# Attention's probabilities times values: plain float32 on halves of the output partitions, and weight buffers at multiples of 256 bytes

## The chip, the cores and the metric

The kernel runs on one core of a Trainium2 chip. The metric is the device time of one execution in microseconds (us). The kernel before takes 1887.37 us, the median of three runs (1886.77 to 1890.65). Besides these there is one profiled execution, from which every row below comes: it took 1884.77 us, and the profile's span of it, from the first to the last instruction, is 1883.0 us.

## The reference

Two layers of a diffusion transformer work on 256 context tokens and 256 latent tokens of width 1024. Each layer has a token mixer (latent attention with 8 heads beside a long convolution called Hyena) and a channel mixer (a dense SwiGLU in layer 0, top 2 of 8 experts in layer 1). All weights and results are float32. The change is inside attention, for each head of 64 values:

```python
def attend(q, k, v):
    s = jnp.einsum('bqhd,bkhd->bhqk', q, k).astype(jnp.float32) * ATTN_SCALE
    p = jax.nn.softmax(s, axis=-1).astype(v.dtype)
    return jnp.einsum('bhqk,bkhd->bqhd', p, v)        # probabilities times values

mix_ctx = ...   # layer 0 only: context queries attend to the 256 context keys
mix_lat = ...   # both layers: latent queries attend to context and latent keys, 512 in all
x = x + g1 * mix_lat
x = x + g2 * channel_mixer(...)   # layer 1: experts' gate, up (1024 x 2816) and down (2816 x 1024), 8 experts
```

So a head of layer 0 has 256 latent queries over 512 keys and 256 context queries over 256 keys; a head of layer 1 has the latent queries alone.

## The kernel before, in words

**Products.** A large matrix product is done as three matmuls on float32r operands, written by `mm3` (L193 to L196). Each operand stands in SBUF as a high part (the value rounded to float32r) and a low part (the rest); the three are high x high (L194), high x low (L195) and low x high (L196). They run on TensorE (PE), whose rows in the trace carry these line numbers. Plain float32 matmuls go through `mm` (L191); the trace shows each of them as two rows. A row of a matmul reads "out<-the operands", then the tile as moving and stationary sizes: 128x512 is a moving operand of 512 columns, and 128\*128 or 128\*2 the stationary one.

**Splitting.** An operand that comes out of a product is split by `split` (L207 on ScalarE, ACT, writes the high part; L209 on VectorE, DVE, the low part). Weights arrive by DMA in `raw` (or `rawx`) and are split by the class `Stream` (L103 on ACT, L105 on DVE) into weight buffers: `hl`, three tiles in the pool `consts`, and later `hlx`, which lie in slots. `fetch` (L87) starts the DMA on SyncE's queue (SP) when a buffer is free.

**Memory.** SBUF holds, one after the other in each partition, the pool `consts` (constants, `raw`, the three `hl`, small things), then 17 slots of 8 KB, then small tiles. Most activations, and in the expert stage the additional weight buffers `hlx`, `rawx`, lie in slots. Worked out from the tile sizes, `hl0` begins at byte 35,776 of a partition and `raw` at byte 19,392 (both 192 past a multiple of 256), and the slots at byte 66,560, a multiple of 256.

**Attention** (`mixer`, L730 on). Layer 0 works on all 512 tokens at once, layer 1 on the 256 latent ones. The loop over heads is written in the order in which PE runs it: for head h the probabilities are transposed (`probs_T`, L951 in the trace) and split into `pt`; then the scores of a later head; a projection of queries and keys for a later pair of heads; a block of Hyena or gate projection (`next_unit`); and the products with the values (`values`). In layer 0 `values(h)` comes after `next_unit`; in layer 1 `values(h - 1)` comes before it. `values` of head h multiplies a block of 128 value columns, which belong to two heads, as the stationary operand with the head's probabilities, 256 queries, as the moving one: 4 key blocks of 128 times 3 matmuls, and in layer 0 the context queries beside them, 2 blocks times 3. Of the 128 output partitions the 64 that belong to the head are kept. The context probabilities stand in `cq` (`ptc`), the values in `vt`, the result in `oT`.

**Elsewhere.** `mod_first`, at the start of layer 0, has float32 matmuls that write output partitions 0 and 1 (operand `mod`) and 64 and 65 (operands `acc` or `mod`) of one PSUM bank; the program's condition vectors `condT` are their stationary operand, two columns wide. `fw` is the network that makes the Hyena filter, also in float32.

Of the kernel before, what the change touches and what calls it, by code (L numbers as in the profile page):

```python
# [8 lines left out]
F32 = mybir.dt.float32  # L9
F32R = mybir.dt.float32r  # L10
# [125 lines left out]
def trunk(ctx, tc, T, out, dump=None, stop=None):  # L136
    nc = tc.nc
    dump = dump or (lambda *a: None)
    consts = ctx.enter_context(tc.tile_pool(name="consts", bufs=1))
# [6 lines left out]
    def nm(s):  # L146
        uid[0] += 1
        return f"{s}_{uid[0]}"
# [3 lines left out]
    def PS(hold=None):  # L152

        k = next(b for b in banks if b not in held)
        banks.remove(k)
        banks.append(k)
        if hold is not None:
            held.add(k)
            hold.append(k)
        return psum.tile([128, 512], F32, name=nm("ps"), tag=f"bank{k}")  # L160
# [14 lines left out]
    def slot(dtype, shape=None, name="s"):  # L175
        k = free.pop(0)
        t = slots.tile([128] + list(shape or [2048]), dtype, name=nm(name), tag=f"slot{k}")
        return Slot(k, t)

    def drop(*ss):  # L180
        for s in ss:
            free.append(s.k)
# [4 lines left out]
    def f(ap):  # L187
        return ap.bitcast(F32)

    def mm(o, l, r, a, b):  # L190
        pe.matmul(o, l, r, start=a, stop=b)  # L191

    def mm3(o, lh, ll, rh, rl, a, b):  # L193
        pe.matmul(o, lh, rh, start=a, stop=False)  # L194
        pe.matmul(o, lh, rl, start=False, stop=False)  # L195
        pe.matmul(o, ll, rh, start=False, stop=b)  # L196

    def copy(i, o, src):
        if i % 2:
            dve.tensor_copy(o, src)  # L200
        else:
            act.activation(o, src, AF.Copy)

    def split(*parts):

        for h, _, src in parts:
            act.activation(h, src, AF.Copy)  # L207
        for h, l, src in parts:
            dve.tensor_tensor(l, src, f(h), OP.subtract)  # L209
# [70 lines left out]
        return vecs[:, l, a:a + n]  # L280


    consts.tile([128, 8], F32, name="fill")
    raw_t = consts.tile([128, 4, 1024], F32, name="raw")
    hl_t = [consts.tile([128, 2, 1024], F32R, name=f"hl{i}") for i in range(3)]
    ri = [0]
# [333 lines left out]
    def split_dft(raw):  # L620
        s = slot(F32R, [2, 2, 512], "dfts")
        split((s.t[:, 0], s.t[:, 1], raw.t))
        drop(raw)
        return s
# [112 lines left out]
    def mixer(l, hTh, hTl, state, hooks, fsteps, in_q=None):  # L737
        N = 512 if l == 0 else 256
        NS = N // 256
        H, L = hT_views(hTh, hTl)  # L740
        qtab = slot(F32, [4, 512], "qtab")
# [35 lines left out]
        def to_T(toks, nb, nk, gain, dst):  # L777
            for kc in range(nk):
                p = PS()
                for tb in range(nb):  # L780
                    pe.transpose(p[:, tb * 128:(tb + 1) * 128], toks[tb][:, kc * 128:(kc + 1) * 128], ident)
                h, lo = dst(kc)
                g = vcol(l, gain + kc)
                act.activation(h, p[:, :nb * 128], AF.Copy, scale=g)
                dve.scalar_tensor_tensor(lo, p[:, :nb * 128], g, f(h), OP.mult, OP.subtract)
# [6 lines left out]
        for tb in range(4):  # L792
            src = kv_ps[tb][:, 256:288]
# [11 lines left out]
        kt = [slot(F32R, [2, 2, 512], "kt") for _ in range(1 + l)]  # L805
# [36 lines left out]
        def unit(c):  # L842
            p = proj_block(("hy", l, c), N)
            if c >= 8:
                short_conv(p, c, x0[0].t[:, c - 8, :N])
                return
            u = tmp("u", [512], bufs=2)
            short_conv(p, c, u[:, :N])
            if c < 4:
                vbuf[c] = u  # L850
            else:
                pool.tensor_tensor(zv[:, c - 4, :N], vbuf.pop(c - 4)[:, :N], u[:, :N], OP.mult)
# [3 lines left out]
        def next_unit():  # L856
            if units:
                unit(units.pop(0))
# [9 lines left out]
        K = state["K"]  # L868
        cq = Pair(N, "cq")
        to_T(cq_tok, N // 128, 3, V_QN, lambda kc: (cq.h[:, kc, :], cq.l[:, kc, :]))  # L870
        vt = [slot(F32R, [4, 512], "vt") for _ in range(2)]
        wh, wl = (t.rearrange("p (k c) -> p k c", k=2) for t in ws.take(("uv", l)))
        for kb in range(4):
            p = PS()
            for kc in range(2):
                mm3(p, ckv.t[:, 0, kc, kb * 128:(kb + 1) * 128], ckv.t[:, 1, kc, kb * 128:(kb + 1) * 128],
                    wh[:, kc], wl[:, kc], kc == 0, kc == 1)
            split((vt[0].t[:, kb, :], vt[1].t[:, kb, :], p))
        qt = slot(F32R, [2, 2, 512], "qt")
        if l == 0:  # L880
            pts = slot(F32R, [2, 4, 256], "pt")
            pt = [(pts.t[:, 0], pts.t[:, 1])]
        else:
            pt = [[x[i].t[:, :, 256:512] for x in (hTh, hTl)] for i in range(2)]
        oT = Pair(N, "oT")

        def qpart(pr):
# [53 lines left out]

        def probs_T(h):
            res = prob.pop(h)
            pth, ptl = pt[h % len(pt)]
            for half in range(2):
                p = PS()
                p3 = p.rearrange("p (k q) -> p k q", k=2)
                for k in range(2):
                    for i in range(2):
                        kb = half * 2 + k  # L950
                        pe.transpose(p3[:, k, i * 128:(i + 1) * 128], res[i][:, kb * 128:(kb + 1) * 128], ident)  # L951
                split((pth[:, half * 2:half * 2 + 2, :], ptl[:, half * 2:half * 2 + 2, :], p3))
            if l == 0:
                p = PS()
                p3 = p.rearrange("p (k q) -> p k q", k=2)
                for k in range(2):
                    for i in range(2):
                        pe.transpose(p3[:, k, i * 128:(i + 1) * 128], res[2][:, i * 256 + k * 128:i * 256 + (k + 1) * 128], ident)
                split((ptc[0], ptc[1], p3))

        def values(h):
            pr, e = divmod(h, 2)
            pth, ptl = pt[h % len(pt)]
            po = PS()
            c = slice(pr * 128, (pr + 1) * 128)
            for kb in range(4):
                mm3(po[:, 0:256], vt[0].t[:, kb, c], vt[1].t[:, kb, c], pth[:, kb, :], ptl[:, kb, :], kb == 0, kb == 3)
            if l == 0:
                for k in range(2):
                    mm3(po[:, 256:512], vt[0].t[:, 2 + k, c], vt[1].t[:, 2 + k, c], ptc[0][:, k], ptc[1][:, k], k == 0, k == 1)  # L970
            r = slice(e * 64, e * 64 + 64)
            split((oT.h[r, pr, :], oT.l[r, pr, :], po[r, :N]))

        if l == 0:
            ptc = [x[:, 3, :].rearrange("p (k q) -> p k q", k=2) for x in (cq.h, cq.l)]
        pairs = {}

        def gate(n, j):
# [27 lines left out]
        for h in range(8):  # L1006
            probs_T(h)
            if h + ahead < 8:
                scores(h + ahead)
            pr = h // 2 + ahead  # L1010
            if h % 2 == 0 and pr < 4:
                proj_pair(pr)
            if h == 4:
                drop(ckv)
                x0.append(slot(F32, [4, 512], "x0"))
            if h == 6:
                drop(qt, *kt)
                if l == 0:
                    drop(qtab)
                else:  # L1020
                    drop(*cq.s)
                Fraw = load_dft("k_fwd", pool, False)
            if h == 7:
                Fd = split_dft(Fraw)
                zts = [slot(F32R, [4, 512], "zt") for _ in range(NS)]
                zt = [zts[0].t, zts[1].t] if l == 0 else [zts[0].t[:, 0:2], zts[0].t[:, 2:4]]
                z_T()
            if l == 0:
                next_unit()
                values(h)  # L1030
            else:
                if h > 0:
                    values(h - 1)
                next_unit()
        if l == 1:
            values(7)
        drop(*vt)
        if l == 0:
            drop(pts, *cq.s)
        dump(f"oT{l}", oT)  # L1040
        dump(f"z{l}", z)

# [5 lines left out]
        for s in range(NS):  # L1048
            yh, yl = slot(F32R, [2, 2, 512], "Yh"), slot(F32R, [2, 2, 512], "Yl")
            Y.append((yh, yl))  # L1050
            for kb in range(2):
                zs = []
                for cs in range(2):
                    p = PS()
# [17 lines left out]
        for j in range(4):  # L1072
            p = PS()
            for s in range(NS):
                i = 0
# [16 lines left out]
        for j in range(8):  # L1092
            ga, gh = [early.pop(n + str(j)) if j < AHEAD[l] else gate(n, j) for n in ("ga", "gh")]
            wh, wl = (t.rearrange("p (b k c) -> p b k c", b=2, k=4) for t in ws.take(("br", l, j)))
            for b, src, g in ((0, oT, ga), (1, oh, gh)):
                p = PS()
# [4 lines left out]
            q, r = divmod(j, 4)  # L1101
# [46 lines left out]

    setup_vectors()
    starts, rows0 = setup_rows()  # L1150
    consts.tile([128, 8], F32, name="end")
    pads.extend(consts.tile([128, 2, 258], F32, name=f"pad{i}") for i in range(2))
    for t in pads:
        dve.memset(t[:, :, 0:258:257], 0.0)
# [53 lines left out]
    hTh, hTl = hT  # L1208
# [33 lines left out]
    hTh, hTl = new  # L1242
# [26 lines left out]
    def mms(p, w, cols):  # L1269
        for kc in range(8):  # L1270
            mm3(p[:, cols], w[0][:, kc], w[1][:, kc], H(kc)[:, cols], L(kc)[:, cols], kc == 0, kc == 7)
# [69 lines left out]
    for hh in range(2):  # L1341
# [15 lines left out]
        else:  # L1357
# [3 lines left out]
            hTh, hTl = alloc_hT()  # L1361
# [146 lines left out]
    for i in range(2):  # L1508
# [3 lines left out]
        for k in range(4):  # L1512
            c = slice(k * 256, (k + 1) * 256)
# [21 lines left out]
    p = PS()  # L1535
# [197 lines left out]
    for b in range(2):  # L1733
        for k in range(2):
            c = slice(k * 512, (k + 1) * 512)
# [25 lines left out]
```

## Time and profile before

| What | Value |
|---|---|
| runs, median (lowest, highest) | 1887.37 us (1886.77, 1890.65) |
| profiled execution | 1884.77 us |
| its span | 1883.0 us |
| granted TensorE clock, mean | 0.993 |
| PE busy | 1827.4 us (97%) |
| VectorE (DVE) busy | 1473.5 us (78%) |
| ScalarE (ACT) busy | 1097.0 us (58%) |
| GpSimd (POOL) busy | 143.2 us (8%) |
| moved by DMA | 436.35 MB, mean 232 GB/s |

An engine's busy time is the part of the span in which an instruction of it was running. The stages follow one another: setup until about 60 us, layer 0's mixer (its attention loop some 120 to 236 us), the dense feed-forward until about 860 us, layer 1's mixer (attention loop some 900 to 955 us), and the experts from about 1075 us to the end.

### The profile page before, as it was taken

To read this page: it belongs to the slowest core of one execution; us is meant where nothing else is said; L and a number is where in the kernel's file an instruction comes from. 1 tells how busy PE (TensorE), PEld (TensorE's weight loads), DVE (VectorE), ACT (ScalarE), POOL (GpSimd) and SP (SyncE) were. 2 spreads that over 40 slices of the span, in tenths; PEclk is the share of its full clock that TensorE was granted. 3 is DMA by queue.
4 is the path that set the end of the run, shared out by engine and by line. 5 is a ranking of instruction groups with operands and counts; after the bars stand their busy time and mean duration, and the time that the engine had idled before them with its cause. 6 is when DMAs were issued, how large, how long until landed. Compare 5 with 4: busy or idle time off the path is not lost. (4 is left out here: it accounts for less than half of the span.)

```text
span 1883.0 us, 25341 instructions
## 1 busy us (share of the span) xinstructions
PE 1827.4 (97%) x9767; PEld 1537.7 (82%) x9767; DVE 1473.5 (78%) x1705; ACT 1097.0 (58%) x1342; POOL 143.2 (8%) x148
## 2 busy tenths in 40 slices
PE   7999999999999999999999899999999999999997
PEld 2888887898888887788999788888878887888785
DVE  5777778787677667768886789888888897888886
ACT  3766633236233235558865577677677676767674
POOL 1122221000000000001221100000000000000000
PEclk9999999999999999999999899999999999999999
DMA  8322226655566676224468499999999999999994
GB/s 296 105 67 67 79 76 199 193 165 144 172 198 191 213 240 204 84 85 117 119 186 262 147 324 339 334 334 342 368 327 344 347 365 324 352 328 360 342 352 180
DMA packets 292316, 436.35 MB, mean 232 GB/s; under 512 B 9848, under 2 KB 162852, under 8 KB 292188
## 3 DMA queue, kind: packets, MB, share of 16 engines
q1 hardware_dynamic: 288652, 422.52, 66.8%
q0 software_dynamic: 3392, 12.00, 2.0%
q8 instruction: 78, 1.28, 0.3%
q14 instruction: 50, 0.41, 0.1%
q10 hardware_dynamic: 144, 0.14, 0.0%
HBM read 433.58 MB, written 1.05 MB: 231 GB/s over the span
## 5 line engine op out<-in xcount | busy, mean ns | idle before, releaser
L103 ACT ACTIVATE hl<-raw 128x1024 fp32r<-128x1024 f32 (+7 forms) x231 | 188.0, 836 | 279.6 <-PE ps L195 167.5
L194 PE MATMUL ps<-hTh,hl 128*128 128x512 f32 (+1 forms) x800 | 283.0, 354 | 0.0
L195 PE MATMUL ps<-hTl,hl 128*128 128x512 f32 (+1 forms) x800 | 283.0, 354 | 0.0
L196 PE MATMUL ps<-hTh,hl 128*128 128x512 f32 (+1 forms) x800 | 282.2, 353 | 0.4 <-DVE hl L105 0.4
L105 DVE TENSOR_TENSOR hl<-raw,hl 128x1024 fp32r<-128x1024 f32 (+7 forms) x231 | 218.7, 965 | 72.0 <-ACT hl L103 71.4
L103 ACT ACTIVATE hlx<-raw 128x2048 fp32r<-128x2048 f32 x124 | 237.9, 1921 | 54.2 <-DMA raw<-in_moe_w_up_dram 16.9
L194 PE MATMUL ps<-hlx,xT 128*128 128x512 f32 (+1 forms) x576 | 215.4, 374 | 0.0
L196 PE MATMUL ps<-hlx,xT 128*128 128x512 f32 (+1 forms) x576 | 214.3, 372 | 0.0
L439 DVE SCALAR_TENSOR_TENSOR acc<-raw,condT,acc 128x1024 f32<-128x1024 f32 x112 | 143.9, 1307 | 36.1 <-DMA raw<-in_w_mod_dram 35.6
L191 PE MATMUL ps<-hlx,aT 128*128 128x512 f32 x704 | 170.2, 393 | 0.0
L196 PEld LDWEIGHTS ps<-hTh,hl 128*128 128x128 f32 x800 | 150.2, 188 | 22.5 <-DVE hl L105 0.6
L194 PEld LDWEIGHTS ps<-hTh,hl 128*128 128x128 f32 x800 | 150.3, 188 | 21.9
L195 PEld LDWEIGHTS ps<-hTl,hl 128*128 128x128 f32 x800 | 150.2, 188 | 20.9
L105 DVE TENSOR_TENSOR hlx<-rawx,hlx 128x2048 fp32r<-128x2048 f32 x65 | 149.3, 2297 | 15.6 <-ACT hlx L103 15.6
L105 DVE TENSOR_TENSOR hlx<-raw,hlx 128x2048 fp32r<-128x2048 f32 x63 | 144.2, 2288 | 16.7 <-ACT hlx L103 16.4
L105 DVE TENSOR_TENSOR hl<-rawx,hl 128x2048 fp32r<-128x2048 f32 (+1 forms) x63 | 141.9, 2254 | 14.3 <-ACT hl L103 13.6
L191 PEld LDWEIGHTS ps<-hlx,aT 128*128 128x128 f32 x704 | 130.1, 188 | 26.3
L105 DVE TENSOR_TENSOR hl<-raw,hlx 128x2048 fp32r<-128x2048 f32 x61 | 139.6, 2288 | 14.4 <-ACT hlx L103 14.4
L195 PE MATMUL ps<-hl,xT 128*128 128x512 f32 (+1 forms) x384 | 146.0, 380 | 3.0 <-DVE hl L105 3.0
L195 PE MATMUL ps<-hlx,xT 128*128 128x512 f32 (+1 forms) x384 | 145.0, 378 | 3.2 <-DVE hlx L105 3.2
L103 ACT ACTIVATE hlx<-rawx 128x2048 fp32r<-128x2048 f32 x67 | 128.4, 1916 | 32.9 <-DMA rawx<-in_moe_w_up_dram 9.1
L103 ACT ACTIVATE hl<-rawx 128x2048 fp32r<-128x2048 f32 (+1 forms) x63 | 118.8, 1888 | 26.7 <-DMA rawx<-in_moe_w_gate_dram 9.9
(395 smaller groups left out, 3749.0 us busy)
## 6 DMA issues: line engine op xcount, KB each, us to landing
rawx<-in_moe_w_gate_dram SPq DMA_DIRECT2D x44, 1024.0 KB
rawx<-in_moe_w_down_dram SPq DMA_DIRECT2D x43, 1024.0 KB
raw<-in_moe_w_down_dram SPq DMA_DIRECT2D x43, 1024.0 KB
raw<-in_moe_w_up_dram SPq DMA_DIRECT2D x42, 1024.0 KB
rawx<-in_moe_w_up_dram SPq DMA_DIRECT2D x41, 1024.0 KB
raw<-in_moe_w_gate_dram SPq DMA_DIRECT2D x41, 1024.0 KB
raw<-in_w_mod_dram SPq DMA_DIRECT2D x80, 512.0 KB
raw<-in_w_in_dram SPq DMA_DIRECT2D x56, 512.0 KB
```

The lines of the kernel that those rows point to most:

```text
L103: self.nc.scalar.activation(a, r, AF.Copy)
L105: self.nc.vector.tensor_tensor(b, r, a.bitcast(F32), OP.subtract)
L191: pe.matmul(o, l, r, start=a, stop=b)
L194: pe.matmul(o, lh, rh, start=a, stop=False)
L195: pe.matmul(o, lh, rl, start=False, stop=False)
L196: pe.matmul(o, ll, rh, start=False, stop=b)
L439: dve.scalar_tensor_tensor(a, raw, condT[:, kc, c:c + 1], a, OP.mult, OP.add)
```

## The change

**Values.** `values` takes a pair of heads. For each key block there is one float32 matmul per head, with the head's own 64 value columns as the stationary operand; head e = 0 of the pair writes output partitions 0 to 63, and e = 1 partitions 64 to 127. Nothing is split for it: `vt`, `pt` and `ptc` are written by one copy each (`copy`, L197 on, alternating between ACT and DVE) in place of a split; the result `oT` is split once per pair on 128 partitions. `pt` holds both heads of a pair in one slot, and `ptc` lies in the free half of `qtab`. In both layers `values` of a pair comes after `next_unit` of its second head.

**Buffers.** The tile `fill` grows by 64 bytes per partition and `end` by 192. By the tile sizes `hl0` begins at byte 35,840 and `raw` at 19,456, both multiples of 256 (as the other two `hl` are, each being 8 KB), and the slots at 66,816, which is again a multiple of 256.

The core of the diff:

```diff
-    consts.tile([128, 8], F32, name="fill")
+    consts.tile([128, 24], F32, name="fill")
...
-        vt = [slot(F32R, [4, 512], "vt") for _ in range(2)]
+        vt = slot(F32, [4, 512], "vt")
...
-            split((vt[0].t[:, kb, :], vt[1].t[:, kb, :], p))
+            copy(kb, vt.t[:, kb, :], p)
...
-        if l == 0:
-            pts = slot(F32R, [2, 4, 256], "pt")
-            pt = [(pts.t[:, 0], pts.t[:, 1])]
-        else:
-            pt = [[x[i].t[:, :, 256:512] for x in (hTh, hTl)] for i in range(2)]
+        pt = slot(F32, [2, 4, 256], "pt")
...
-                split((pth[:, half * 2:half * 2 + 2, :], ptl[:, half * 2:half * 2 + 2, :], p3))
+                copy(half, pt.t[:, h % 2, half * 2:half * 2 + 2, :], p3)
...
-                split((ptc[0], ptc[1], p3))
+                copy(h, ptc[h % 2], p3)
...
-        def values(h):
-            pr, e = divmod(h, 2)
-            pth, ptl = pt[h % len(pt)]
+        def values(pr):
+
             po = PS()
-            c = slice(pr * 128, (pr + 1) * 128)
+
+            def mms(q, src, kb, a, b):
+                for e in range(2):
+                    c = pr * 128 + e * 64
+                    mm(po[e * 64:e * 64 + 64, q], vt.t[:, kb, c:c + 64], src(pr * 2 + e), a, b)
             for kb in range(4):
-                mm3(po[:, 0:256], vt[0].t[:, kb, c], vt[1].t[:, kb, c], pth[:, kb, :], ptl[:, kb, :], kb == 0, kb == 3)
+                mms(slice(0, 256), lambda h: pt.t[:, h % 2, kb, :], kb, kb == 0, kb == 3)
             if l == 0:
                 for k in range(2):
-                    mm3(po[:, 256:512], vt[0].t[:, 2 + k, c], vt[1].t[:, 2 + k, c], ptc[0][:, k], ptc[1][:, k], k == 0, k == 1)
-            r = slice(e * 64, e * 64 + 64)
-            split((oT.h[r, pr, :], oT.l[r, pr, :], po[r, :N]))
+                    mms(slice(256, 512), lambda h: ptc[h % 2][:, k], 2 + k, k == 0, k == 1)
+            split((oT.h[:, pr, :], oT.l[:, pr, :], po[:, :N]))
...
-            if l == 0:
-                next_unit()
-                values(h)
-            else:
-                if h > 0:
-                    values(h - 1)
-                next_unit()
-        if l == 1:
-            values(7)
+            next_unit()
+            if h % 2:
+                values(h // 2)
...
-    consts.tile([128, 8], F32, name="end")
+    consts.tile([128, 56], F32, name="end")
```

On PE in layer 0, the end of a head's Hyena block, its values and the next head's transposes; before, the last six of the 18 value matmuls of one head (`ps_1282` is the output, `pt` and `cq` the probabilities):

```order
L196 MATMUL ps_1282<-pt_969,vt_928 128x256
L194 MATMUL ps_1282<-cq_904,vt_927 128x256
L195 MATMUL ps_1282<-cq_905,vt_927 128x256
L196 MATMUL ps_1282<-cq_904,vt_928 128x256
L194 MATMUL ps_1282<-cq_904,vt_927 128x256
L195 MATMUL ps_1282<-cq_905,vt_927 128x256
L196 MATMUL ps_1282<-cq_904,vt_928 128x256
L951 MATMUL ps_1303<-misc,P_1177 128x128
```

After, at the end of the second head of a pair, the whole of the pair's values stands between the block (`hTh`, `hTl`) and the transposes (64x256 gives the tile's stationary columns and moving columns; the line of the transposes is L946 now):

```order
L194 MATMUL ps_1331<-hTh_278,hl_84 128x512
L195 MATMUL ps_1331<-hTl_280,hl_84 128x512
L196 MATMUL ps_1331<-hTh_278,hl_84 128x512
L191 MATMUL ps_1363<-pt_964,vt_927 64x256 x8
L191 MATMUL ps_1363<-qtab_425,vt_927 64x256 x4
L946 MATMUL ps_1378<-misc,P_1314 128x128
L946 MATMUL ps_1378<-misc,P_1318 128x128
```

The 36 float32r matmuls of two heads have become 12 float32 ones in one place.

On DVE in layer 1, at the end of the loop over heads, what stands ahead of the low part of `zt` (the Hyena branch's input, which PE needs first after the loop) and behind it; before:

```order
L209 TENSOR_TENSOR dfts_8138<-dft_8074,dfts_8138 128x1024
L209 TENSOR_TENSOR hTl_6617<-ps_8060,hTh_6615 128x2x256
L209 TENSOR_TENSOR hTl_6617<-ps_8067,hTh_6615 128x2x256
L209 TENSOR_TENSOR oT_7245<-ps_8076,oT_7245 64x256
L105 TENSOR_TENSOR hl_83<-raw,hl_83 128x1024
L105 TENSOR_TENSOR hl_84<-raw,hl_84 128x1024
L209 TENSOR_TENSOR hTl_6618<-ps_8124,hTh_6616 128x2x256
L209 TENSOR_TENSOR hTl_6618<-ps_8131,hTh_6616 128x2x256
L209 TENSOR_TENSOR zt_8141<-ps_8142,zt_8141 128x512
L209 TENSOR_TENSOR zt_8141<-ps_8149,zt_8141 128x512
L209 TENSOR_TENSOR oT_7245<-ps_8156,oT_7245 64x256
```

After:

```order
L200 COPY pt_7103<-ps_7871 128x512
L209 TENSOR_TENSOR dfts_7924<-dft_7877,dfts_7924 128x1024
L105 TENSOR_TENSOR hl_84<-raw,hl_84 128x1024
L200 COPY pt_7103<-ps_7918 128x512
L209 TENSOR_TENSOR zt_7927<-ps_7928,zt_7927 128x512
L209 TENSOR_TENSOR zt_7927<-ps_7935,zt_7927 128x512
L105 TENSOR_TENSOR hl_85<-raw,hl_85 128x1024
L209 TENSOR_TENSOR oT_7104<-ps_7975,oT_7104 128x256
```

Four splits of probabilities (written into halves of `hTl` before) have become two copies, and one `oT` stands after `zt` only.

## Rows read from the trace of the kernel before

**Rows 1.** Windows; columns: stretch, its us, each engine's busy us, PEclk, DMA share, GB/s:
```profile
120.00:236.00 116.00, 116.00 (x658) 101.38 (x657) 85.89 (x190) 78.11 (x170) 30.84 (x28) 1.00 0.24 68
900.00:955.00 55.00, 55.00 (x422) 52.59 (x421) 46.11 (x96) 41.10 (x85) 17.85 (x24) 1.00 0.43 118
1200.00:1860.00 660.00, 650.73 (x3119) 537.18 (x3118) 553.95 (x336) 472.76 (x339) 0.00 (x0) 1.00 0.95 343
```

**Rows 2.** Timeline, PE, layer 0, one head's values; columns: start, us, engine, line:
```profile
140.41 0.28 PE L194 MATMUL ps<-pt,vt 128*128 128x256 f32 x1
...
142.57 1.04 PE L951 MATMUL ps<-misc,P 128*128 128x128 f32 x8
```

**Rows 3.** Timeline, PE, layer 1, one head's values:
```profile
900.71 0.28 PE L194 MATMUL ps<-hTh,vt 128*128 128x256 f32 x1
...
902.13 0.28 PE L194 MATMUL ps<-hTh,hl 128*128 128x256 f32 x1
```

**Rows 4.** Timeline, PE, float32 among float32r in setup:
```profile
35.27 0.29 PE L196 MATMUL ps<-hl,hTl 128*128 128x288 f32 x1
35.39 0.29 PE L194 MATMUL ps<-hl,hTh 128*128 128x288 f32 x1
35.62 1.02 PE L191 MATMUL ps<-mod,condT 128*2 128x512 f32 x2
36.57 0.41 PE L195 MATMUL ps<-hl,hTh 128*128 128x288 f32 x1
```

**Rows 5.** Timeline, PE, float32 of 256 columns in the filter network:
```profile
66.42 0.61 PE L191 MATMUL ps<-fw 64*64 64x256 f32 x2 [0.70 <-DVE P L772]
66.96 0.44 PE L196 MATMUL ps<-hl,hTl 128*128 128x384 f32 x1
```

**Rows 6.** Timeline, PE, `mod_first`, output partitions 0, 1 and 64, 65:
```profile
23.14 0.59 PE L191 MATMUL ps<-acc,sel 128*2 128x512 f32 x1
23.15 0.59 PE L191 MATMUL ps<-mod,condT 128*2 128x512 f32 x1
...
26.24 1.89 PE L191 MATMUL ps<-mod,condT 128*2 128x512 f32 x8
```

**Rows 7.** Tile `fw`, weight loads on PE (PEld), 66 to 67 us:
```profile
L191 PEld LDWEIGHTS ps<-fw x2: 129/131/133, 66.4 to 66.4; 64*64 64x64 f32 x2
```

**Rows 8.** Timeline, PE, experts' down product, 512 columns:
```profile
1746.81 7.44 PE L191 MATMUL ps<-hlx,aT 128*128 128x512 f32 x32
1754.09 3.89 PE L191 MATMUL ps<-hl,aT 128*128 128x512 f32 x16
1757.82 7.44 PE L191 MATMUL ps<-hlx,aT 128*128 128x512 f32 x32
```

**Rows 9.** Timeline, PE, experts' gate and up, 256 columns:
```profile
1827.97 0.28 PE L194 MATMUL ps<-hl,xT 128*128 128x256 f32 x1
...
1830.69 0.28 PE L194 MATMUL ps<-hlx,xT 128*128 128x256 f32 x1
```

**Rows 10.** Tile `hl`, its matmuls; ns min/median/max, first and last start us:
```profile
L191 PE MATMUL ps<-hl,aT x352: 388/394/483, 1138.0 to 1866.7; 128*128 128x512 f32 x176
L194 PE MATMUL ps<-hl,xT x192: 275/393/398, 1080.8 to 1830.3; 128*128 128x512 f32 x160, 128*128 128x256 f32 x32
L195 PE MATMUL ps<-hl,xT x384: 276/393/504, 1078.3 to 1830.5; 128*128 128x512 f32 x160, 128*128 128x256 f32 x32
L194 PE MATMUL ps<-hl,asp x160: 392/394/503, 695.3 to 832.8; 128*128 128x512 f32 x160
L194 PE MATMUL ps<-hl,mT x160: 276/281/367, 388.6 to 1053.9; 128*128 128x256 f32 x160
```

**Rows 11.** Timeline, PE, layer 1's output projection, 256 columns:
```profile
1042.90 0.28 PE L194 MATMUL ps<-hl,mT 128*128 128x256 f32 x1
...
1046.67 0.28 PE L196 MATMUL ps<-hl,mT 128*128 128x256 f32 x1
```

**Rows 12.** Waits of SP's queue, 1060 to 1870 us; us in total, times, longest:
```profile
SPq L87 <- DVE hl L105: 325.9, 121, 8.2
```

More of the change, by code (lines that the diff above doesn't have):

```diff
@@ L958, in probs_T @@
                         pe.transpose(p3[:, k, i * 128:(i + 1) * 128], res[2][:, i * 256 + k * 128:i * 256 + (k + 1) * 128], ident)
-                split((ptc[0], ptc[1], p3))
-        def values(h):
-            pr, e = divmod(h, 2)
-            pth, ptl = pt[h % len(pt)]
+                copy(h, ptc[h % 2], p3)
+        def values(pr):
             po = PS()
-            c = slice(pr * 128, (pr + 1) * 128)
+            def mms(q, src, kb, a, b):
+                for e in range(2):
+                    c = pr * 128 + e * 64
+                    mm(po[e * 64:e * 64 + 64, q], vt.t[:, kb, c:c + 64], src(pr * 2 + e), a, b)
             for kb in range(4):
-                mm3(po[:, 0:256], vt[0].t[:, kb, c], vt[1].t[:, kb, c], pth[:, kb, :], ptl[:, kb, :], kb == 0, kb == 3)
+                mms(slice(0, 256), lambda h: pt.t[:, h % 2, kb, :], kb, kb == 0, kb == 3)
             if l == 0:
                 for k in range(2):
-                    mm3(po[:, 256:512], vt[0].t[:, 2 + k, c], vt[1].t[:, 2 + k, c], ptc[0][:, k], ptc[1][:, k], k == 0, k == 1)
-            r = slice(e * 64, e * 64 + 64)
-            split((oT.h[r, pr, :], oT.l[r, pr, :], po[r, :N]))
+                    mms(slice(256, 512), lambda h: ptc[h % 2][:, k], 2 + k, k == 0, k == 1)
+            split((oT.h[:, pr, :], oT.l[:, pr, :], po[:, :N]))
         if l == 0:
-            ptc = [x[:, 3, :].rearrange("p (k q) -> p k q", k=2) for x in (cq.h, cq.l)]
+            ptc = [qtab.t[:, 2 + e].rearrange("p (k q) -> p k q", k=2) for e in range(2)]
         pairs = {}
@@ L1016, in mixer @@
             if h == 6:
-                drop(qt, *kt)
-                if l == 0:
-                    drop(qtab)
-                else:
-                    drop(*cq.s)
+                drop(qt, *kt, *cq.s)
                 Fraw = load_dft("k_fwd", pool, False)
@@ L1027, in mixer @@
                 z_T()
-            if l == 0:
-                next_unit()
-                values(h)
-            else:
-                if h > 0:
-                    values(h - 1)
-                next_unit()
-        if l == 1:
-            values(7)
-        drop(*vt)
+            next_unit()
+            if h % 2:
+                values(h // 2)
+        drop(vt, pt)
         if l == 0:
-            drop(pts, *cq.s)
+            drop(qtab)
         dump(f"oT{l}", oT)
```

## The prediction, made before the changed kernel ran

> **What bounds the kernel now.** I read the windows first, then the timeline of PE around the values, then waits. In the stretch of layer 0's attention loop the reader is to see PE busy for 116.00 of 116.00 us, in layer 1's for 55.00 of 55.00, and in the experts for 650.73 of 660.00, at a granted clock of 1.00 throughout [rows 1]. DVE and ACT have gaps in all three stretches. So PE bounds the kernel: in both loops what shortens or lengthens PE's own rows moves the end by as much, and what is taken from DVE or ACT moves nothing. In the experts there is a second limit close behind, the transfers at a share of 0.95 [rows 1]; they are held by the buffers, since SP's queue waits 325.9 us for `hl` to be split [rows 12], and a buffer comes free when PE is done with it.
>
> The sum is made against the profiled execution, 1884.77 us (span 1883.0 us); the median of the runs lies 2.6 us above it. I move both by the same amount.
>
> **Values, before.** A head of layer 0 takes 18 rows from 140.41 to 142.57 us, 2.16 us or 0.120 us each [rows 2]; eight heads take 17.3 us. A head of layer 1 takes 12 rows from 900.71 to 902.13, 1.42 us or 0.118 us each [rows 3]; eight take 11.4 us. No idle time stands in these rows.
>
> **Values, after.** A pair of layer 0 takes 12 float32 matmuls, a pair of layer 1 takes 8, each of them two rows in the trace, of 256 columns. The price of a row comes from two float32 rows of 512 columns in 1.02 us, where one alone takes 0.59 [rows 4, 6]: 1.02 - 0.59 = 0.43 us from one to the next, so 0.215 for 256 columns. The nearest row of that width agrees: two rows of 256 columns begin at 66.42, and the next instruction at 66.96, so 0.54 us, which is 2 x 0.215 and 0.11 for the change of form [rows 5].
>
> Do the two halves run at once? `mod_first` writes partitions 0, 1 and 64, 65 from stationary operands of two columns. A row of the one (`acc`) begins at 23.14 and a row of the other (`mod`) at 23.15, each 0.59 us long; and eight rows, which alternate between the halves, take 1.89 us [rows 6]. One after another they would take 7 x 0.43 + 0.59 = 3.60; in pairs 3 x 0.43 + 0.59 = 1.88. So two rows share a step there. The values' halves have 64 columns rather than 2, and two moving operands from SBUF at a time, as `acc` and `mod` are two; I take a step of 0.215 us for two rows.
>
> The change of form costs something at each group. Before the float32 rows of setup the distance is 0.23 us (35.39 to 35.62) where it was 0.12 (35.27 to 35.39), and behind them 36.57 - 35.62 - 2 x 0.43 = 0.09 [rows 4]: 0.11 + 0.09 = 0.20 us a group, and there are eight groups. The row shows that a change of form costs 0.1 us either way. The Trainium skill, page "TensorEngine Tiling (Array Packing)", section Tiling Modes (Key Properties), says that a change of the tiling mode drains the engine, which speaks against this change; by it each change would cost the tail of a row, 0.59 - 0.43 = 0.16 us, 2.6 us over the 16 changes where the sum below has 1.6, so the sum would be 1 us smaller.
>
> Layer 0: four pairs of 12 x 0.215 + 0.20 = 2.78 us, 11.1 in all, against 17.3: -6.2. Layer 1: four pairs of 8 x 0.215 + 0.20 = 1.92 us, 7.7 in all, against 11.4: -3.7. **Together -9.9 us.** Bounds: both halves in turn, +7.4 (rival B); weight loads that don't keep up, -6.2 (rival C); a change of form that costs nothing, -11.5.
>
> **The rest of the values' edit** I cost at nothing. Three splits a head in layer 0 and two in layer 1 become copies, which frees about half their time on ACT and DVE; PE doesn't wait for these in either loop [rows 1]. Order: `values` of a pair now stands behind the block of the second head, so its probabilities are older by a block than they need be in layer 1. The next transposes overwrite half of `pt` only after their copy, which comes behind the transposes on PE, and these behind the values that read it. At the end of layer 1's loop PE needs `zt`; its cover on PE shrinks by one head's values, about 1 us, while DVE has two copies in place of four splits ahead of it, as the order of DVE shows. That is what would be late next, and the cover there is a block of 24 rows at 0.12 and the last values, 4.8 us, for two splits. `oT` is split after the last values and read first after the whole Hyena branch. SP's and POOL's issues stand in the order in which they stood.
>
> **Buffers.** No row before has `hl` at a multiple of 256, but `hlx`, at one, does the same work beside it. At 512 moving columns 16 rows of `hl` take 1754.09 to 1757.82, 0.2331 us each, and 32 rows of `hlx` 1746.81 to 1754.09, 0.2275 [rows 8]: -5.6 ns a row if the place is the reason. In the experts `hl` is the moving operand of 352 rows with `aT` and 768 with `xT` (192 + 384 + 192, the third line as the first), five in six of these at 512 columns by the forms, so 992 rows [rows 10]: -5.6 us. In the feed-forward there are 3 x 160 with `asp` [rows 10]: -2.7 us. At 256 columns the place seems to work the other way: 24 rows of `hl` take 1827.97 to 1830.69, 0.113 us each [rows 9], from a row of `mT` at 1042.90 to the 32nd after it at 1046.67 it is 0.118 [rows 11], while values from slots take 0.120 [rows 2]. That would be +6.7 ns on 128 rows, 0.9 us, in the experts, +2.2 ns on 480 rows of `mT`, 1.1 us, and, if stationary operands go the same way, as much on about 1,080 rows of layer 1's mixer, 2.2 us. In front of the experts: -2.7 + 1.1 + 2.2 = +0.6. In the experts: -5.6 + 0.9 = -4.7, of which I count half, because the transfers are at 0.95 and PE cannot run ahead of them for long: -2.4. **Together -1.8 us.** Bounds: all of the gain at 512 and no loss, -8.3; the losses alone, +4.2. Of this the row shows only two buffers that differ in more than their place. The Trainium skill, page "SBUF — State Buffer", section Specifications (TRN2), gives lines of 16 bytes; both old and new places are multiples of that, so by the page nothing would change here (rival D, whose price is worked out without it).
>
> **Sum:** -9.9 - 1.8 = -11.7 us. The profiled execution would be 1873.1 us, the median 1887.4 - 11.7 = **1875.7 us**.
>
> **Rivals.**
>
> A, the forecast: 1875.7 us, chance 0.50.
>
> B, the halves take turns. For it: the two-row overlap was seen with stationary operands of two columns only, and two streams of float32 at full length might share one path. Against it: rows 6, in which the streams are as long. Layer 0 would take 24 x 0.215 + 0.20 = 5.36 us a pair against 4.32, layer 1 16 x 0.215 + 0.20 = 3.64 against 2.84: 4 x 1.04 + 4 x 0.80 = +7.4. With the buffers 1887.4 + 7.4 - 1.8 = 1893.0 us. It decides from the point where a step of two rows exceeds some 0.35 us, at which the values cost what they did. Chance 0.08.
>
> C, weight loads set the step. A load of 64 columns takes 129 to 133 ns [rows 7], and a step has two, 0.26 us, if loads of the two halves follow each other and are repeated for each row. Layer 0: 12 x 0.26 + 0.20 = 3.32 us a pair, layer 1: 2.28; so 17.3 - 13.3 + 11.4 - 9.1 = 6.3 less than before. With the buffers -8.1, 1879.3 us. Chance 0.12.
>
> D, the place of the buffers does nothing, and `hl` and `hlx` differ for another reason (what else runs beside them). -9.9 alone, 1877.5 us. For it: 256 and 512 columns contradict each other in sign. Chance 0.20.
>
> E, the place gives all of the gain at 512 columns and the other differences aren't its doing; transfers follow, because it is the buffers that hold them. -9.9 - 8.3 = -18.2, 1869.2 us. Chance 0.10.
>
> **How the numbers follow.** About 0.2% (3.8 us) is what a measurement of this kernel can tell from no change. A, D and E are faster by more, 0.80 together, and C by most of its width, so faster has 0.85. Of C with the buffers' losses in full (-6.3 + 4.2 = -2.1) and of a B cut by half, 0.07 are within 0.2%; the rest, 0.08, is B, slower. The range reaches from somewhat below E to the forecast with all the buffers' losses (1887.4 - 9.9 + 4.2 = 1881.7) and a little of C: 1867 to 1883 us. Outside lie B, a part of C, and gains larger than any worked out.
>
> **What would show it.** In the profile after: the eight groups of float32 values, each with pairs of rows that begin within 0.02 us of each other and follow at 0.215 us; about 2.8 us from the first of a group to the transposes in layer 0 and 1.9 us in layer 1. Rows that start one by one at 0.215 mean B, pairs at 0.26 mean C. `hl,aT` rows at 0.2275 confirm the place, at 0.233 refute it (D); `mT` rows above 0.118 confirm the loss. In the experts a shorter span at a DMA share above 0.95 says that transfers followed. PE busy for all of both loops would confirm that no wait came in; an idle gap on PE before the first rows with `zt` in layer 1 would show the cover gone. Wrong would be the forecast if the loops got shorter and the stages behind them longer by as much, that is, if something other than PE carried the time across.

## The result, and the profile after

The changed kernel takes 1871.82 us, the median of six runs (1863.88 to 1877.18), beside 1887.59 for the kernel before (six runs): -15.8 us by the medians. The ratio is 0.991 with a 95% interval of 0.988 to 0.994, which is -17 us (-22 to -12). Forecast were -11.7 us and 1875.7, with a range of 1867 to 1883. The profiled execution took 1873.24 us; its span is 1871.4 us, against 1883.0.

The changed kernel's own runs differ by 13 us and go for the most part with the clock: the two at a mean granted TensorE clock of 0.994 and 0.995 took 1863.88 and 1864.09 us, the four at 0.991 and 0.992 took 1871.69 to 1877.18. A difference of a few us between two single executions is therefore no evidence, and the reasons below rest on the distance from one matmul to the next.

Windows of the profile after, shifted to the same work as in [rows 1] for the two loops:

```profile
118.00:232.00 114.00, 114.00 (x627) 93.04 (x626) 81.54 (x176) 74.61 (x158) 32.97 (x28) 1.00 0.26 70
890.00:945.00 55.00, 55.00 (x407) 48.58 (x406) 43.27 (x86) 38.51 (x77) 18.71 (x25) 1.00 0.43 118
1200.00:1860.00 660.00, 648.91 (x3103) 538.86 (x3101) 551.83 (x337) 465.67 (x336) 0.00 (x0) 0.99 0.93 338
```

PE is still busy for all of both loops: no wait came in. In the experts the clock reads 0.99 where it was 1.00, and this comes from short stretches. The first window is of the changed kernel behind the end of an expert, the second of the kernel before at the same place:

```profile
1353.00:1358.00 5.00, 4.25 (x12) 3.33 (x13) 5.00 (x5) 3.57 (x4) 0.00 (x0) 0.66 0.62 202
```

```profile
1366.00:1371.00 5.00, 4.25 (x18) 3.50 (x19) 5.00 (x5) 3.58 (x4) 0.00 (x0) 1.00 0.64 211
```

Both lie behind a place where one expert follows another and PE waits about 1 us for `yh`; 12 matmuls in place of 18 is what the lower clock (0.66 on average, the 1.2 GHz level for some 3.4 us of the five) costs here. This execution had three such stretches at such places in the experts, the one of the kernel before had none there, and two further executions of the changed kernel, profiled below, had one and two. So it changes from one execution to the next of the same kernel, and no difference is explained by it.

Layer 0's values of a pair, which answer to [rows 2]:

```profile
148.98 0.39 PE L196 MATMUL ps<-hTh,hl 128*128 128x512 f32 x1
149.30 1.95 PE L191 MATMUL ps<-pt,vt 128*64 128x256 f32 x16
151.08 1.03 PE L191 MATMUL ps<-qtab,vt 128*64 128x256 f32 x8
152.04 0.44 PE L946 MATMUL ps<-misc,P 128*128 128x128 f32 x2
```

From 149.30 to 152.04 the 24 rows take 2.74 us, 2.78 forecast with the change of form: 16 rows of 0.38 us in 1.95, so two at a time. The row ahead takes 0.32 us to the next start rather than 0.23, as at the change of form in [rows 4].

Layer 1's last pair, which answers to [rows 3]:

```profile
933.27 0.28 PE L196 MATMUL ps<-hTh,hl 128*128 128x256 f32 x1
933.48 1.95 PE L191 MATMUL ps<-pt,vt 128*64 128x256 f32 x16
935.36 0.50 PE L194 MATMUL ps<-zt,dfts 128*128 128x512 f32 x1
```

The 16 rows take 1.88 us, and the first row with `zt` follows without an idle time: the cover held.

The experts' down product, which answers to [rows 8]:

```profile
1734.00 7.42 PE L191 MATMUL ps<-hlx,aT 128*128 128x512 f32 x32
1741.25 3.79 PE L191 MATMUL ps<-hl,aT 128*128 128x512 f32 x16
1744.88 7.42 PE L191 MATMUL ps<-hlx,aT 128*128 128x512 f32 x32
```

The 16 rows with `hl` take 3.63 us, 0.2269 each, where they took 0.2331: now as fast as `hlx` (7.25 / 32 = 0.2266).

At 256 columns, the gate and up rows that answer to [rows 9], 24 of `hl`:

```profile
1816.18 0.28 PE L194 MATMUL ps<-hl,xT 128*128 128x256 f32 x1
...
1819.05 0.28 PE L194 MATMUL ps<-hlx,xT 128*128 128x256 f32 x1
```

2.87 / 24 = 0.120 us, where it was 0.113: the short rows became slower, as forecast. So did the rows with `mT`, which answer to [rows 11]; from one to the 32nd after it:

```profile
1032.11 0.28 PE L194 MATMUL ps<-hl,mT 128*128 128x256 f32 x1
...
1035.95 0.28 PE L196 MATMUL ps<-hl,mT 128*128 128x256 f32 x1
```

3.84 / 32 = 0.120 us, where it was 0.118.

### The profile page after: what moved, and what is told of

Read it like the earlier page. It is cut to its first block, busy times and chain, and to the rows that moved or that the text cites. A ratio compares the mean times of both kernels' runs of the same rounds, so it can differ in the third digit from the quotient of the medians.

```text
span 1871.4 us, 25084 instructions
## 1 busy us (share of the span) xinstructions
PE 1815.1 (97%) x9687; PEld 1527.7 (82%) x9687; DVE 1461.6 (78%) x1673; ACT 1081.8 (58%) x1310; POOL 145.1 (8%) x148
```

## The experiments

All runs of the kernel before in one set are shared; the ratio is to them, with its 95% interval. Spacings are from one start to the next on PE in the profiled execution.

**The buffers alone.** The kernel before, with

```diff
-    consts.tile([128, 8], F32, name="fill")
+    consts.tile([128, 24], F32, name="fill")
...
-    consts.tile([128, 8], F32, name="end")
+    consts.tile([128, 56], F32, name="end")
```

> The kernel before with the two tiles fill and end enlarged as in the change, nothing else. Theory: the place of the weight buffers is a gain of its own: rows of 512 columns with hl follow at 0.227 us where they took 0.229 to 0.233, rows of 256 columns with hl at 0.120 where they took 0.114 to 0.118. By the classes of rows in the two traces that is -12 us at 512 and +6 us at 256 columns, so -6 us, some 1881.5 where before takes 1887.5. Rival: hl was slower for what ran beside it, and the place does nothing: 0 us, spacings as before, and the change's whole gain is the values'.

Measured: 1877.27 us, the kernel before in that set 1885.66; ratio 0.9943 (0.9925 to 0.9962), -10.8 us (-14.1 to -7.2). The place does much, and the rival is refuted. By the mean spacing of each class of rows, times its number, the effect is -7.9 us: -4.0 on the 1,896 rows with `hl` stationary at 512 columns, 1,872 of which are in layer 0 (0.2290 to 0.2269), -3.2 on the 528 rows with `hl` moving ahead of the experts, -5.3 on the 992 in the experts, -1.6 on the other rows of 512 columns, mostly with `hlx`, some of which alternate with rows of `hl`, and +6.2 on the rows of 256 columns, half of it (+3.0) on the 936 of layer 1 with `hl` stationary (0.1168 to 0.1199).

**The values alone.** The changed kernel, with

```diff
-    consts.tile([128, 24], F32, name="fill")
+    consts.tile([128, 8], F32, name="fill")
...
-    consts.tile([128, 56], F32, name="end")
+    consts.tile([128, 8], F32, name="end")
```

> The changed kernel with fill and end at their old sizes, so hl at 192 past a multiple of 256. Theory: the values alone give what their groups show in the trace after, -5.7 us in layer 0 and -3.6 in layer 1: -9.3 us, some 1878; rows of hl at 512 columns follow at 0.229 to 0.233 us again. Rival (place does nothing): -16 us as the whole change.

Measured: 1879.44 us; ratio 0.9956 (0.9942 to 0.9971), -8.3 us (-10.9 to -5.5). The rows of the experts are slow again, 3.73 us for 16:

```profile
1736.52 3.89 PE L191 MATMUL ps<-hl,aT 128*128 128x512 f32 x16
1740.25 7.44 PE L191 MATMUL ps<-hlx,aT 128*128 128x512 f32 x32
```

**The change again, in the same set.** No edit.

> The changed kernel once more, beside the two halves of the change on the same chip. Theory: the two halves add up, -15 to -16 us, 1872. Rival (the places matter less when the values are short, or the gain at 512 columns is handed back in the experts): less than the sum of the two by 3 us or more.

Measured: 1868.47 us; ratio 0.990 (0.988 to 0.9921), -18.9 us (-22.6 to -14.9). The two halves give -10.8 - 8.3 = -19.1: they add up.

From profiled executions of the four kernels (the first two columns are those of the profiles above), between the same two matmuls of the program in each (us; less the time that a granted clock below 1.00 took in the window, its length times one minus the clock, where it was below). The windows of the two loops also take in some us of matmuls beside the loop:

| Stage | before | change | buffers alone | values alone |
|---|---|---|---|---|
| layer 0's attention loop | 134.7 | 128.8 | 134.1 | 129.1 |
| layer 0's second half and the feed-forward, up to layer 1's loop | 665.0 | 660.3 | 659.9 | 663.6 |
| layer 1's attention loop | 69.2 | 66.5 | 70.0 | 65.6 |
| experts | 800.9 | 794.5 | 792.7 | 797.2 |

The values act in the two loops (-5.6 and -3.6 us alone), the buffers mostly outside them and, in layer 1's loop, the other way (+0.8). In the second row and in the experts the values alone have nothing to act on, and their -1.4 and -3.7 there show how far two executions can be apart in these stages.

**The halves in turn.** The changed kernel, with all matmuls of one head before those of the other:

```diff
-            def mms(q, src, kb, a, b):
-                for e in range(2):
...
+            for e in range(2):
+                c, o = pr * 128 + e * 64, po[e * 64:e * 64 + 64]
+                for kb in range(4):
+                    mm(o[:, 0:256], vt.t[:, kb, c:c + 64], pt.t[:, e, kb, :], kb == 0, kb == 3)
+                if l == 0:
+                    for k in range(2):
+                        mm(o[:, 256:512], vt.t[:, 2 + k, c:c + 64], ptc[e][:, k], k == 0, k == 1)
```

> The changed kernel with the values of a pair written in turn: all matmuls of head e = 0, then all of e = 1, so that rows next to each other use the same half. Theory: only neighbouring rows of different halves share a step; in turn each row takes a step of 0.21 us, so layer 0 has 24 steps where the change has 12 (+2.5 us a pair), layer 1 16 where it has 8 (+1.7 us a pair): +16.8 us over the change, 1888.5. Rival: PE holds rows of the two halves apart in queues and runs them side by side in whatever order they stand: no difference.

Measured: 1878.87 us, +10.4 over the change in its set; ratio 0.996 (0.9945 to 0.9976). Neither was right: most steps are single, but not all. Layer 0, the timeline where the first head ends (`qtab`) and the second begins (`pt`):

```profile
151.71 1.03 PE L191 MATMUL ps<-pt,vt 128*64 128x256 f32 x4
152.57 0.38 PE L191 MATMUL ps<-qtab,vt 128*64 128x256 f32 x1
152.58 0.43 PE L191 MATMUL ps<-pt,vt 128*64 128x256 f32 x1
152.79 0.38 PE L191 MATMUL ps<-qtab,vt 128*64 128x256 f32 x1
152.85 0.38 PE L191 MATMUL ps<-pt,vt 128*64 128x256 f32 x1
153.01 0.38 PE L191 MATMUL ps<-qtab,vt 128*64 128x256 f32 x1
153.06 0.38 PE L191 MATMUL ps<-pt,vt 128*64 128x256 f32 x1
153.22 0.38 PE L191 MATMUL ps<-qtab,vt 128*64 128x256 f32 x1
153.28 1.24 PE L191 MATMUL ps<-pt,vt 128*64 128x256 f32 x5
154.36 1.03 PE L191 MATMUL ps<-qtab,vt 128*64 128x256 f32 x4
155.32 0.55 PE L946 MATMUL ps<-misc,P 128*128 128x128 f32 x3
```

The first row of the second head starts at 152.58, beside the first head's ninth of twelve, so four rows of the two overlap, and 24 rows take 20 steps: 4.52 us a pair where the change takes 2.74, and 2.79 against 1.88 in layer 1. 4 x 1.78 + 4 x 0.91 = 10.8 us, and 10.4 were measured. So the overlap is real, it is worth that much, and here PE started a row of the other half four rows ahead of its turn. The eight groups in turn take 4 x 4.52 + 4 x 2.79 = 29.2 us, beside 28.9 for the values before: in this order the values' edit gains nothing, and what is left of this run's gain (0.996, some -7.5 us) is the buffers'.

**`hl` at 64 and at 128.** The changed kernel, the slots unmoved, with (first 64, then 128)

```diff
-    consts.tile([128, 24], F32, name="fill")
+    consts.tile([128, 40], F32, name="fill")
...
-    consts.tile([128, 56], F32, name="end")
+    consts.tile([128, 40], F32, name="end")
```

```diff
-    consts.tile([128, 24], F32, name="fill")
+    consts.tile([128, 56], F32, name="fill")
...
-    consts.tile([128, 56], F32, name="end")
+    consts.tile([128, 24], F32, name="end")
```

> The changed kernel with hl at 64 past a multiple of 256 (fill 40, end 40; the slots stay). Theory: at 512 columns a row is fast (0.227 us) only where both operands begin at a multiple of 256, so rows with hl go back to 0.229 to 0.233 and rows of 256 columns to 0.114 to 0.118: +6 us over the change, 1878. Rival: it takes only a multiple of 64, and 192 was slow for being the odd one of the four: as the change, 1872.

> The changed kernel with hl at 128 past a multiple of 256 (fill 56, end 24; the slots stay). Theory (multiples of 256 count): as with 64, +6 us, 1878. Rival (multiples of 128 count): as the change, 1872.

Measured, the kernel before in that set 1888.99: at 64 1882.13 us, ratio 0.997 (0.9959 to 0.9982); at 128 1886.54 us, 0.9982 (0.9971 to 0.9993). Beside the change's ratio of 0.990 to 0.991 that is 11 to 13 and 14 to 16 us slower: multiples of 64 or 128 don't do, but the theory had the size wrong. At 64, rows with `hl` moving and then 24 rows with `hl` stationary in layer 0:

```profile
1347.91 3.84 PE L191 MATMUL ps<-hl,aT 128*128 128x512 f32 x16
1351.59 7.44 PE L191 MATMUL ps<-hlx,aT 128*128 128x512 f32 x32
```

```profile
120.55 0.40 PE L194 MATMUL ps<-hTh,hl 128*128 128x512 f32 x1
...
126.15 1.03 PE L946 MATMUL ps<-misc,P 128*128 128x128 f32 x8
```

3.68 / 16 = 0.230 with `hl` moving, and 5.60 / 24 = 0.233 with `hl` stationary. In the kernel before it was the other way about, 0.233 moving [rows 8] and 5.49 / 24 = 0.229 stationary, in the same 24 rows:

```profile
120.52 0.39 PE L194 MATMUL ps<-hTh,hl 128*128 128x512 f32 x1
...
126.01 1.04 PE L951 MATMUL ps<-misc,P 128*128 128x128 f32 x8
```

At 128 the moving ones are at 0.2325:

```profile
1342.95 3.88 PE L191 MATMUL ps<-hl,aT 128*128 128x512 f32 x16
1346.67 7.43 PE L191 MATMUL ps<-hlx,aT 128*128 128x512 f32 x32
```

**The slots at 64.** The changed kernel, with

```diff
-    consts.tile([128, 56], F32, name="end")
+    consts.tile([128, 8], F32, name="end")
```

> The changed kernel with the slots at 64 past a multiple of 256 and hl at a multiple (end 8). Theory (both operands must begin at a multiple of 256): nearly every matmul has an operand in a slot; rows of 512 columns between slots, 2,055 of them in the experts, would rise from 0.228 to 0.229 to 0.233, some +6 to +10 us there and as much in the stages before, less up to 6 us at 256 columns: +5 to +12 us, 1877 to 1884. Rival (only the operand from hl counts, by what else lies near it): no difference, 1872.

Measured: 1876.79 us; ratio 0.994 (0.9924 to 0.9955), 6 to 8 us slower than the change. Neither account holds: rows between slots stay at 0.227 though both operands have left the multiples of 256 (7.28 / 32 below), and the rows with `hl`, which stands at a multiple, are at 0.2331, those of the kernel before.

```profile
1736.39 7.44 PE L191 MATMUL ps<-hlx,aT 128*128 128x512 f32 x32
1743.67 3.89 PE L191 MATMUL ps<-hl,aT 128*128 128x512 f32 x16
1747.40 7.44 PE L191 MATMUL ps<-hlx,aT 128*128 128x512 f32 x32
```

The rows with `hl` stationary are those of the kernel before, too, 5.49 / 24 = 0.229:

```profile
122.70 0.39 PE L194 MATMUL ps<-hTh,hl 128*128 128x512 f32 x1
...
128.19 1.04 PE L946 MATMUL ps<-misc,P 128*128 128x128 f32 x8
```

This gave the theory of the next set: what counts is how far the moving operand begins from the stationary one, modulo 256.

**Both at 192, and `hl` at 32.** The changed kernel, with (first both, then `hl` alone)

```diff
-    consts.tile([128, 24], F32, name="fill")
+    consts.tile([128, 8], F32, name="fill")
```

```diff
-    consts.tile([128, 24], F32, name="fill")
+    consts.tile([128, 32], F32, name="fill")
...
-    consts.tile([128, 56], F32, name="end")
+    consts.tile([128, 48], F32, name="end")
```

> The changed kernel with hl at 192 past a multiple of 256, as in the kernel before, and the slots at 192 past one too (fill 8, end 56). Theory: what counts is the distance between the starts of a matmul's two operands, modulo 256, and not the place of either: here it is 0 for every matmul, so rows of 512 columns with hl follow at 0.227 us and rows of 256 columns at 0.120, as in the change: the change's time within 2 us. Rival (multiples of 256 count): rows with hl at 0.229 to 0.235 us, and those between slots as well, some 10 us or more over the change.

> The changed kernel with hl at 32 past a multiple of 256 (fill 32, end 48; the slots stay). Theory: a distance of 32 lies between 0 and 64, so moving hl rows of 512 columns between 0.227 and 0.229 us and stationary ones between 0.227 and 0.235: 2 to 8 us over the change. Rival (the distance is taken in steps of 64): rows as in the change, the change's time.

> The changed kernel on the same chip as these two, as their measure: 1868 to 1872 us.

Measured, the kernel before in that set 1885.32: both at 192, 1871.73 us, ratio 0.9919 (0.9898 to 0.9939); the change 1868.56, 0.991 (0.9895 to 0.9924); `hl` at 32, 1887.46, 1.0013 (1.0004 to 1.0023). With both at 192 the rows are those of the change, 3.63 us for 16:

```profile
1743.31 3.79 PE L191 MATMUL ps<-hl,aT 128*128 128x512 f32 x16
1746.94 7.42 PE L191 MATMUL ps<-hlx,aT 128*128 128x512 f32 x32
```

So a multiple of 256 isn't needed, an equal remainder is. The time is that of the change as far as these runs can tell: 0.0009 in the ratio is 1.7 us, within both intervals. `raw`, which ACT and DVE read, moves along with `hl` in these runs, and its place isn't the cause: with the slots at 64 it stands where the change has it, and the rows with `hl` are slow; with both at 192 it stands where the kernel before has it, and they are fast. At 32 the rows with `hl` moving are the slowest of those measured, 3.74 / 16 = 0.2337, and the values' whole gain is gone:

```profile
1352.14 3.90 PE L191 MATMUL ps<-hl,aT 128*128 128x512 f32 x16
1355.88 7.45 PE L191 MATMUL ps<-hlx,aT 128*128 128x512 f32 x32
```

The expected loss of 2 to 8 us was too small: the spacing doesn't rise steadily with the distance.

**`hl` at both places.** The changed kernel, with a second set of views of the weight buffers, 192 bytes further, for layer 1's mixer:

```diff
-    hl_t = [consts.tile([128, 2, 1024], F32R, name=f"hl{i}") for i in range(3)]
+    hl_all = consts.tile([128, 3 * 2048 + 48], F32R, name="hl")
+    hl_t, hl_u = ([hl_all[:, o + i * 2048:o + (i + 1) * 2048].rearrange("p (a b) -> p a b", a=2) for i in range(3)] for o in (0, 48))
...
-        h, l = buf.h[:, :n], buf.l[:, :n]
+        h, l = buf.alt if buf.alt and len(key) > 2 and key[1] == 1 and key[0] in ("hy", "uv", "qk", "ga", "gh", "br", "out") else (buf.h, buf.l)
+        h, l = h[:, :n], l[:, :n]
...
-    consts.tile([128, 56], F32, name="end")
+    consts.tile([128, 8], F32, name="end")
```

> The changed kernel with the weights of layer 1's mixer, apart from the q, kv and uv products, placed 192 bytes further in the same buffers: hl at 192 past a multiple of 256 where the rows have 256 columns, at a multiple of 256 in all other stages. Theory: layer 1's 936 rows with hl stationary and 160 with hl moving go from 0.120 back to 0.117 and 0.115 us, -3.6 us, the rest stays: 1868. Rival: the short rows depend on something else than the place of hl: 1872. A wait for the shared bytes where the layers meet could cost up to 1 us.

The views overlap by 192 bytes, so where the two placements follow each other some weights are overwritten, and part of the products uses other numbers than the reference's; the amount of work is the same. Measured in the second set: 1872.38 us, ratio 0.9913 (0.9896 to 0.993). The short rows of layer 1 did go down, from 0.1199 to 0.1175 with `hl` stationary and from 0.1197 to 0.1167 with it moving, 2.2 and 0.6 us by their number, but the run is no faster than the change as far as this can be told: inconclusive. A version without the overlap needs 3 x 192 = 576 bytes more a partition and was not tried.

## Why the prediction came out as it did

**PE bounds both loops:** right. The loops became shorter by what PE's own rows lost, and no wait came in.

**Values, -9.9 us:** right. By rows -9.3: eight heads of layer 0 took 17.25 us and four pairs take 4 x (2.74 + 0.09 ahead + 0.05 in the transposes behind) = 11.5, so -5.7; layer 1 goes from 11.63 to 8.1, -3.6. The step of two rows is 0.216 us (0.215 forecast). Alone the edit gives -8.3 (-10.9 to -5.5). Rival B fell with the pairs, whose rows begin 0.007 us apart, and with the halves in turn; rival C with the step, which is below the 0.26 us of two weight loads.

**A change of form, 0.20 us a group:** right, 0.19: 0.09 ahead of it, 0.05 more in the transposes behind, and a first step of 0.266 rather than 0.216. A cost of 0.16 us at each of the two changes of a group would have been 0.32.

**Buffers, -1.8 us:** the sign was right, the size wrong, and this is the term in which the forecast missed. The rows give -7.9, the experiment -10.8 (-14.1 to -7.2), at or beyond the lower of the bounds that the forecast gave this term (-8.3 and +4.2). Three parts of it were off.

- Rows with `hl` stationary at 512 columns were left out; 0.0021 us on 1,872 of them is -3.9. Rows with `hlx` in the experts, which it didn't count either, gave another -1.4.
- Half of the gain in the experts was discounted, "because the transfers are at 0.95", 2.4 of 4.7 us by the forecast's own rows; by the measured rows the gain there is 6.0. With the buffers alone the experts take 8.2 us less than before and 4.5 less than with the values alone. Single executions differ too much in this stage for one pair to settle it, but the other profiles can be added. From the first matmul with `P,h` to the last with `yh,P`, corrected for the clock as in the table, the seven executions in which `hl` shares the slots' remainder there (the change three times, buffers alone, in turn, both places, both at 192) average 795.6 us (793.8 to 797.2), and the three with `hl` moving at a distance of 192 (before, values alone, slots at 64) average 799.6 (798.1 to 801.7). That is 4.0 us: more than the forecast let through, less than the rows add up to. So most of the gain came through, and whether transfers held back the rest isn't shown. The sign that the prediction named for it, a DMA share above 0.95, wasn't seen: the window of the profile after has 0.93.
- The loss at 256 columns was 6.2 rather than 4.2, which went the other way. Part of it is a slip in the sum: +2.2 ns on 1,080 rows is 2.4 us and not 2.2.

**Rival D (the place does nothing)** is refuted by the buffers alone. **Rival E** came near the measured total (-18.2), but by luck: it had the gain on the rows with `hl` moving at 512 columns (8.3 forecast, 8.5 by the rows), and the two things that it missed, -5.6 on the other rows of 512 columns and the loss of 6.2 at 256, nearly cancel. It is luck, too, that the profiled execution took 1873.24 us where the forecast had 1873.1: it was among the changed kernel's slower ones, and had three stretches at the lower clock in the experts.

With the measured terms the sum is -9.3 - 7.9 = -17.2 us, against a measured -17 by the first ratio and -18.9 and -17.0 in the two repeats.

## What to carry to other kernels

Where PE is busy without a gap, float32 matmuls that use half of the output partitions can replace three float32r ones, if neighbours in the program alternate between the halves: here it was the order that made 24 rows cost 12 steps and not 20, and with 20 there was no gain. Lay moving and stationary operands out so that their start addresses leave the same remainder modulo 256 bytes when the moving operand has 512 float32r columns, and read the spacing of matmuls by buffer before trusting an allocation: 32 bytes more in front of the weights cost the whole gain of this change. A DMA share of 0.95 wasn't a wall here, where SP's queue waits for buffers [rows 12]: with faster rows on PE the stage took some 4 us less.

## What the runs showed of the hardware

In these runs the spacing of float32r matmuls of 512 columns goes by the distance from the stationary operand's start to the moving one's, modulo 256 bytes, whichever of the two buffers is shifted: `hl` 192 further (before) and the slots 64 further (slots at 64) make the same distances, 192 with `hl` moving and 64 with `hl` stationary, and the same spacings. The column for `hl` moving is from 16 rows of `hl,aT`, that for `hl` stationary the mean over the 1,872 rows of layer 0:

| Distance, bytes | `hl` moving, us | `hl` stationary, us |
|---|---|---|
| 0 | 0.227 (change; both at 192) | 0.227 (change; both at 192) |
| 32 | 0.234 (`hl` at 32) | |
| 64 | 0.230 (`hl` at 64) | 0.229 (before; slots at 64) |
| 128 | 0.2325 (`hl` at 128) | 0.233 (`hl` at 128) |
| 192 | 0.233 (before; slots at 64) | 0.233 (`hl` at 64) |
| 224 | | 0.233 (`hl` at 32) |

At 256 columns it goes the other way: 0.120 us at distance 0, and 0.113 to 0.118 at 64 and 192. Why is open: the runs don't tell whether the moving reads meet the weight load for the next matmul or something else, and no run here moved one operand within its buffer.

Two float32 rows of 256 columns on different halves of the output partitions begin 0.007 us apart and share a step of 0.216 us, although the record of one weight load of 64 columns is 0.13 to 0.14 us long.
